# A two-block network on one core: attention of the second block regrouped by head pair, and its PSUM banks dealt out anew

## The chip, the cores and the metric

The kernel runs on one core of one Trainium2 chip. Its time is the device time of one execution in microseconds (us), and of several executions the median is taken. [...] VectorE (DVE) and ScalarE (ACT) read PSUM and do all element-wise work, and the queue of SyncE (SP) fetches the weights from memory.

## The reference

A first block (gating, dilated attention, and a mixture of 16,384 one-row experts) is followed by the two layers of the second block. The change touches these two layers alone. One layer is, cut to what matters (256 tokens, width 1024, eight heads of 64 in each half):

```python
def hybrid_layer(x, w_in, w_out, ln_g, ln_b, rel_bias, topk):
    proj = jnp.einsum('bsd,dn->bsn', x, w_in)
    qA, kA, vA, gA, qB, kB, vB, gB, qI, kI, wI = jnp.split(proj, SPLIT_POINTS, axis=-1)
    oA = stick_breaking_attention(heads(qA), heads(kA), heads(vA))
    oB = dsa_sparse_attention(heads(qB), heads(kB), heads(vB), qI, kI, wI, rel_bias, topk)
    mix = jnp.concatenate([oA * jax.nn.silu(gA), oB * jax.nn.silu(gB)], axis=-1)
    y = jnp.einsum('bsm,md->bsd', mix, w_out)
    return layer_norm_2(ALPHA * x + y, ln_g, ln_b)
```

Half A ("stick") weighs a key by the sigmoid of its score times a running product over the keys between. Half B ("selected") keeps for each query the 64 keys with the highest index score and takes a softmax over them with a position bias.

## The kernel before, in words

All weights and activations are split into a high and a low part, and each product is three matrix multiplications (L116 to L118: high by high, high by low, low by high). A weight arrives as a unit of 128x1024 (`raw`). ACT rounds it to its high part `uhi` (L98) and DVE subtracts to get the low part `ulo` (L99). Seven buffer pairs for split units are used in turn, so that splitting can run ahead of PE by up to seven units.

Two forms of projection appear. With `w_stationary` the weights are the stationary operand: one unit gives 24 matrix multiplications of 256 columns into one PSUM tile `pp`, which ACT then copies out; `heads_t` (L776 to L781) does this for the index projections and for the queries and keys of both halves, one unit per head pair, and the same loop at L847 to L851 for the gates. With `x_units` the tokens are stationary: one unit gives 12 matrix multiplications of 512 columns, six for each block of 128 tokens (`tb`). The values (`rows`, L798) and the output projection at the end (L935 to L941) are made in this form.

One layer runs in the program as follows: values of half B; index keys and queries; index scores (L821) and the choice of 64 keys on DVE (L834 to L844); the gates; then queries and keys of half B (L860, L861); half B for four head pairs (L863 to L891); queries, keys and values of half A (L895 to L897); half A for four head pairs (L900 to L932); the output projection; and the layer norm by token block (L942 to L964), which in the first layer also transposes the result for the next one (L960, L163).

Half B, for one head pair: scores (L788); mask, add and row maximum on DVE (L871); four exponentials on ACT (L875); scaling on DVE (L879); six transposes (L886); a copy (L888); the product with the values, `weighted` (L795); and `finish`, which multiplies by the gate on DVE (L856) and splits the result into `mh` and `ml` (L98, L99). Half A, for one head pair: scores and mask (L905 to L910); Abs, Exp and Ln on ACT (L913 to L915); one DVE step (L917); a split into `sh` and `sl`; products with a triangle (L923) and with minus one (L926), added onto the scores in the same PSUM tile; Exp (L929); `weighted` (L795); and `finish`.

PSUM in this part: `banks()` gives a tile `mm` of two banks, of which there are two in turn, for scores and transposes alike. The rest is three single banks `pp` and one bank `po` for the result of `weighted`. The output projection has four accumulators of one bank, for two halves of the columns (`n`) by two token blocks: those of `n` = 0 are the two banks of one `mm` tile, those of `n` = 1 are two `pp` tiles (L935, L936).

```python
            bk = banks()
            acc4 = [[bk[:, tb, :] for tb in range(2)], [ps_b.tile([128, 512], F32, name="pp") for _ in range(2)]]
```

The order of each engine's instructions is fixed when the program is built. A planner walks the instructions in program order with costs of its own and lets a later one pass one that would still wait, so that the order on an engine isn't the program's. [...]

Of the kernel before, what the change touches and what calls it, by code (L numbers as in the profile page):

```python
# [9 lines left out]
F32 = mybir.dt.float32  # L10
# [5 lines left out]
AF = mybir.ActivationFunctionType  # L16
ALU = mybir.AluOpType
AX = mybir.AxisListType
PSUM = bass.MemoryType.PSUM
# [5 lines left out]
KD = 8  # L25
# [13 lines left out]
def kernel(  # L39
# [146 lines left out]
    def w_stationary(ps, xh, xl, src, eng=V):  # L186
        hi, lo = unit(src, eng)
        for k in range(KD):
            s = slice(k * 128, (k + 1) * 128)
            end = mm3(ps, hi[:, s], lo[:, s], xh[:, k, :], xl[:, k, :], k == 0, k == KD - 1)  # L190
        return end
# [540 lines left out]
    with ExitStack() as c4:  # L732
        p2 = c4.enter_context(tc.tile_pool(name="p2", bufs=1))
        w2 = c4.enter_context(tc.tile_pool(name="w2", bufs=2))
        ps_m = c4.enter_context(tc.tile_pool(name="ps_m2", bufs=2, space=PSUM))


        def banks():
            return ps_m.tile([128, 2, 512], F32, name="mm")

        for tb in range(2):
            bk = banks()
            for n in range(2):
# [10 lines left out]
        cv.close()  # L754
        ps_b = c4.enter_context(tc.tile_pool(name="ps_b2", bufs=3, space=PSUM, side="right"))
        cur = x2
# [15 lines left out]
        for layer in range(2):  # L772
            blk = [0]
            qI = p2.tile([128, 4, T], F32, name="qI", tag="q")

            def heads_t(dst, scale=1.0, func=AF.Copy):  # L776
                for j in range(dst.shape[1]):
                    pp = ps_b.tile([128, T], F32, name="pp")
                    w_stationary(pp, xh, xl, w_t[layer, blk[0]])
                    blk[0] += 1  # L780
                    S.activation(out=dst[:, j, :], in_=pp, func=func, scale=scale)  # L781
# [8 lines left out]

            def weighted(po, v, hp, w):
                for sb, t in ((0, slice(0, 256)), (1, slice(128, 256))):
                    for e in range(2):
                        h = 2 * hp + e
                        P.matmul(out=po[64 * e:64 * e + 64, t], lhsT=v[:, sb, h * 64:(h + 1) * 64],  # L795
                                 rhs=w[:, e, 256 * sb:256 + 128 * sb], start=(sb == 0), stop=(sb == 1))

# [11 lines left out]
            with tc.issue_after(x_ready):  # L809
                heads_t(kI[:, None, :])  # L810
            pw = ps_b.tile([128, 512], F32, name="pp")[:, 0:256].rearrange("p (b t) -> p b t", b=2)
# [4 lines left out]
            with tc.issue_after(x_ready):  # L816
                heads_t(qI)


            acc = [w2.tile([128, T], F32, name=f"acc{tb}", bufs=1) for tb in range(2)]  # L820
            for hp in range(4):  # L821
                pss = banks()
                both_heads(pss, qI, hp, lambda s, sl: kI[s, 0:sl])
# [22 lines left out]

            for k in range(KD):  # L847
                pp = ps_b.tile([128, T], F32, name="pp")
                w_stationary(pp, xh, xl, w_t[layer, blk[0]])
                blk[0] += 1  # L850
                S.activation(out=gT[:, k, :], in_=pp, func=AF.Silu)  # L851
            exp_ln_set()

            def finish(k, po):
                mx_ = w2.tile([128, T], F32, name="mix")
                V.tensor_tensor(out=mx_, in0=po, in1=gT[:, k, :], op=ALU.mult)  # L856
                split(mh[:, k, :], ml[:, k, :], mx_)


            heads_t(qB, 0.125)  # L860
            heads_t(kB)  # L861

            for hp in range(4):  # L863
                pss = banks()
                both_heads(pss, qB, hp, lambda s, sl: kB[s, hp, 0:sl])
# [12 lines left out]
                for e, tb, n in each:  # L878
                    V.tensor_scalar(out=sm[:, e, COL[tb]], in0=sm[:, e, COL[tb]], scalar1=ls[:, n:n + 1],  # L879
                                    scalar2=None, op0=ALU.mult)  # L880
                pt = banks()
                for e in range(2):
# [5 lines left out]
                V.tensor_copy(out=pT, in_=pt[:, :, 0:384])  # L888
                po = ps_b.tile([128, T], F32, name="po", bufs=1)
                weighted(po, vB, hp, pT)  # L890
                finish(4 + hp, po)  # L891


            qA = p2.tile([128, 4, T], F32, name="qA", tag="q")
            heads_t(qA, 0.125)  # L895
            heads_t(kA)
            rows(vA, 0)  # L897


            for hp in range(4):  # L900
                z = banks()
                zz = z[:, :, 0:384]
# [22 lines left out]
                for e in range(2):  # L925
# [3 lines left out]
                S.activation(out=aw, in_=zz, func=AF.Exp)  # L929
                po = ps_b.tile([128, T], F32, name="po", bufs=1)  # L930
                weighted(po, vA, hp, aw)
                finish(hp, po)  # L932


            bk = banks()  # L935
            acc4 = [[bk[:, tb, :] for tb in range(2)], [ps_b.tile([128, 512], F32, name="pp") for _ in range(2)]]  # L936
            parts = [(acc4[n] + [4, 2], w_out_2[layer, n * 4 + i], 2 * i)
                     for i, n in ((2, 1), (3, 1), (2, 0), (3, 0), (0, 0), (1, 0), (0, 1), (1, 1))]
            for j in range(4):
                x_units(parts[j:j + 1], mh, ml)  # L940
            x_units(parts[4:], mh, ml)  # L941
            for tb in range(2):  # L942
                bk = banks() if layer == 0 else None
                st = small.tile([128, 2, 6], F32, name="st2")
# [106 lines left out]
```

## Time and profile before

| | |
|---|---|
| median of three runs | 1301.3 us (1301.26 to 1305.01) |
| the profiled execution | 1302.54 us, of which its span 1300.4 us |
| PE busy in the span | 1256.5 us (97%) |
| DVE, ACT busy | 974.0 us (75%), 641.4 us (49%) |
| the second block | from about 953 us to the end |

A busy share is an average over very different stages. The rows below come from the views of the stages that the change touches: stretches in which all of PE's work is projections, stretches in which attention is mixed in, the step from the first to the second layer, and the end. In the timeline a row gives start and length, engine, line, operation, and output and inputs; in square brackets stands how long the engine sat idle before it, and on whom it waited. Rows of PE overlap, since matrix multiplications are pipelined: what one costs is the distance to the next start. A group's row gives count, busy time, mean length of one in ns, and the idle time before them with its releaser.

### The profile page before, as it was taken

The numbers are of one execution on the slowest core, as the hardware profiler recorded it, in microseconds if no ns is written. First come the engines' busy times: TensorE is split into PE (matmuls) and PEld (weight loads), VectorE is DVE, ScalarE is ACT, GpSimd is POOL, SyncE is SP. The second block draws the span as 40 slices with busy tenths as digits, with TensorE's granted clock in tenths as the row PEclk, the third lists the DMA queues.
The fourth block names the chain that finished last, engine by engine and source line by source line (L and its number), as shares of the span: only waits on it lengthen the run. The fifth ranks groups of instructions, "written<-read, shape, count | busy, mean of one in ns | idle before, by whom it ended". The sixth has DMA issues, their size and how long they took to land. (4 is left out here: it accounts for less than half of the span.)

```text
span 1300.4 us, 22723 instructions
## 1 busy us (share of the span) xinstructions
PE 1256.5 (97%) x8888; PEld 1111.3 (85%) x8888; DVE 974.0 (75%) x1907; ACT 641.4 (49%) x1031; POOL 14.8 (1%) x27
## 2 busy tenths in 40 slices
PE   7999999999999999999999999999999999899995
PEld 5777998999999999998888887888879986699874
DVE  6977999944557999989999987655569665667744
ACT  7555554444544444444444446445455546355561
POOL 0001000000000000000000000000000000000000
PEclk9999999999999999999999999999999999899998
DMA  7824454565564545555555558755654532346310
GB/s 254 263 90 133 149 172 165 180 196 187 172 200 164 164 163 163 164 176 169 177 176 177 178 178 285 245 191 184 192 185 148 181 128 91 130 164 196 122 56 32
DMA packets 61818, 219.08 MB, mean 168 GB/s; under 512 B 7064, under 2 KB 8496, under 8 KB 61584
## 3 DMA queue, kind: packets, MB, share of 16 engines
q1 hardware_dynamic: 60272, 213.03, 49.3%
q0 software_dynamic: 1440, 4.62, 1.2%
q8 instruction: 69, 1.13, 0.3%
q14 instruction: 37, 0.30, 0.1%
HBM read 214.33 MB, written 3.16 MB: 167 GB/s over the span
## 5 line engine op out<-in xcount | busy, mean ns | idle before, releaser
L99 DVE TENSOR_TENSOR ulo<-raw,uhi 128x1024 fp32r<-128x1024 f32 x390 | 474.6, 1220 | 180.8 <-ACT uhi L98 180.2
L98 ACT ACTIVATE uhi<-raw 128x1024 fp32r<-128x1024 f32 x390 | 411.3, 1056 | 360.6 <-PE pu L117 205.3
L116 PE MATMUL pu<-xh,uhi 128*128 128x256 f32 x1024 | 293.5, 287 | 2.3 <-ACT ga L462 2.3
L118 PE MATMUL pu<-xh,ulo 128*128 128x256 f32 x1024 | 292.1, 285 | 1.6 <-DVE ulo L99 1.5
L117 PE MATMUL pu<-xl,uhi 128*128 128x256 f32 x1024 | 290.3, 284 | 0.0
L116 PE MATMUL pv<-uhi,wh 128*128 128x512 f32 x512 | 203.6, 398 | 0.0
L118 PE MATMUL pv<-uhi,wl 128*128 128x512 f32 x512 | 200.8, 392 | 0.5 <-DVE wl L99 0.4
L116 PEld LDWEIGHTS pu<-xh,uhi 128*128 128x128 f32 x1024 | 197.0, 192 | 3.9 <-ACT ga L462 3.1
L117 PE MATMUL pv<-ulo,wh 128*128 128x512 f32 x512 | 200.3, 391 | 0.0
L118 PEld LDWEIGHTS pu<-xh,ulo 128*128 128x128 f32 x1024 | 197.1, 192 | 3.3 <-DVE ulo L99 2.6
L117 PEld LDWEIGHTS pu<-xl,uhi 128*128 128x128 f32 x1024 | 197.2, 193 | 0.0
L116 PE MATMUL pp<-xh,uhi 128*128 128x256 f32 x496 | 141.1, 284 | 0.0
L117 PE MATMUL pp<-xl,uhi 128*128 128x256 f32 x496 | 140.5, 283 | 0.0
L118 PE MATMUL pp<-xh,ulo 128*128 128x256 f32 x496 | 140.1, 282 | 0.0
L98 ACT ACTIVATE wh<-ga 128x256 fp32r<-128x256 f32 x128 | 53.0, 417 | 174.5 <-PE pv L117 172.5
L118 PEld LDWEIGHTS pv<-uhi,wl 128*128 128x128 f32 x512 | 96.1, 188 | 23.5 <-DVE wl L99 1.8
L117 PEld LDWEIGHTS pv<-ulo,wh 128*128 128x128 f32 x512 | 96.2, 188 | 20.2
L116 PEld LDWEIGHTS pv<-uhi,wh 128*128 128x128 f32 x512 | 96.1, 188 | 19.8
L116 PEld LDWEIGHTS pp<-xh,uhi 128*128 128x128 f32 x496 | 94.0, 189 | 3.1 <-issue 3.0
L117 PEld LDWEIGHTS pp<-xl,uhi 128*128 128x128 f32 x496 | 93.9, 189 | 1.5 <-issue 1.4
L118 PEld LDWEIGHTS pp<-xh,ulo 128*128 128x128 f32 x496 | 94.0, 190 | 0.7 <-issue 0.7
L659 DVE SCALAR_TENSOR_TENSOR ga<-pg,ga 128x288 f32<-128x288 f32 (+1 forms) x96 | 87.1, 937 | 7.3 <-PE pg L657 7.3
(278 smaller groups left out, 1653.2 us busy)
## 6 DMA issues: line engine op xcount, KB each, us to landing
raw<-in_expert_u_dram SPq DMA_DIRECT2D x128, 512.0 KB, 3.4
raw<-in_expert_v_dram SPq DMA_DIRECT2D x128, 512.0 KB, 3.3
raw<-in_w_t_dram SPq DMA_DIRECT2D x58, 512.0 KB, 3.9
raw<-in_w_out_dram SPq DMA_DIRECT2D x24, 512.0 KB, 3.3
raw<-in_w_in_n_dram SPq DMA_DIRECT2D x16, 512.0 KB, 5.1
raw<-in_w_n_dram SPq DMA_DIRECT2D x16, 512.0 KB, 3.4
raw<-in_w_query_dram SPq DMA_DIRECT2D x12, 512.0 KB, 3.6
raw<-in_w_in_t_dram SPq DMA_DIRECT2D x4, 512.0 KB, 4.5
```

What stands on the lines that cost most here:

```text
L98: S.activation(out=hi, in_=src, func=AF.Copy)
L99: eng.tensor_tensor(out=lo, in0=src, in1=hi.bitcast(F32), op=ALU.subtract)
L116: P.matmul(out=ps, lhsT=lh, rhs=rh, start=start, stop=False)
L117: P.matmul(out=ps, lhsT=lh, rhs=rl, start=False, stop=False)
L118: return P.matmul(out=ps, lhsT=ll, rhs=rh, start=False, stop=stop).ins
L659: V.scalar_tensor_tensor(out=gv, in0=pg, scalar=1.0 / 32768.0, in1=gv, op0=ALU.mult, op1=ALU.mult)
```

## The change

Both halves are taken head pair by head pair in one loop, each behind its own query and key projection: values of A; then for each pair queries and keys of A, `stick`, queries and keys of B, `selected`. `heads_t` takes the place of its units as an argument, so that they can be read out of order.

PSUM is dealt out otherwise. Half A has one two-bank tile for itself (`mm0`) and half B one (`mm1`), each single-buffered. `po` is gone: `weighted` writes its result into the last 128 columns of the two banks that the pair is using, in three pieces of 128 columns for each head instead of one of 256 and one of 128. The bank so freed is a fourth `pp`. All four accumulators of the output projection are now `pp` tiles of their own. Its units come in another order.

```diff
-        ps_m = c4.enter_context(tc.tile_pool(name="ps_m2", bufs=2, space=PSUM))
-        def banks():
-            return ps_m.tile([128, 2, 512], F32, name="mm")
+        ps_m = c4.enter_context(tc.tile_pool(name="ps_m2", bufs=1, space=PSUM))
+        def banks(n):
+            return ps_m.tile([128, 2, 512], F32, name="mm", tag=f"mm{n % 2}")
...
-        ps_b = c4.enter_context(tc.tile_pool(name="ps_b2", bufs=3, space=PSUM, side="right"))
+        ps_b = c4.enter_context(tc.tile_pool(name="ps_b2", bufs=4, space=PSUM, side="right"))
...
-            def heads_t(dst, scale=1.0, func=AF.Copy):
-                for j in range(dst.shape[1]):
+            def heads_t(dst, base, scale=1.0, func=AF.Copy, js=None):
+                for j in (range(dst.shape[1]) if js is None else js):
                     pp = ps_b.tile([128, T], F32, name="pp")
-                    w_stationary(pp, xh, xl, w_t[layer, blk[0]])
-                    blk[0] += 1
+                    w_stationary(pp, xh, xl, w_t[layer, base + j])
                     S.activation(out=dst[:, j, :], in_=pp, func=func, scale=scale)
...
-            def weighted(po, v, hp, w):
-                for sb, t in ((0, slice(0, 256)), (1, slice(128, 256))):
+            def weighted(bk, v, hp, w):
+                po = bk[:, :, 384:512]
+                for n, (tb, sb) in enumerate(((0, 0), (1, 0), (1, 1))):
                     for e in range(2):
                         h = 2 * hp + e
-                        P.matmul(out=po[64 * e:64 * e + 64, t], lhsT=v[:, sb, h * 64:(h + 1) * 64],
-                                 rhs=w[:, e, 256 * sb:256 + 128 * sb], start=(sb == 0), stop=(sb == 1))
+                        P.matmul(out=po[64 * e:64 * e + 64, tb, :], lhsT=v[:, sb, h * 64:(h + 1) * 64],
+                                 rhs=w[:, e, n * 128:(n + 1) * 128], start=(sb == 0), stop=(sb == tb))
+                return po
...
-            heads_t(qB, 0.125)
-            heads_t(kB)
-            for hp in range(4):
-                pss = banks()
+            def selected(hp):
+                pss = banks(1)
...
-                pt = banks()
+                pt = banks(1)
...
-                po = ps_b.tile([128, T], F32, name="po", bufs=1)
-                weighted(po, vB, hp, pT)
-                finish(4 + hp, po)
-            qA = p2.tile([128, 4, T], F32, name="qA", tag="q")
-            heads_t(qA, 0.125)
-            heads_t(kA)
-            rows(vA, 0)
-            for hp in range(4):
-                z = banks()
+                finish(4 + hp, weighted(pt, vB, hp, pT))
+            def stick(hp):
+                z = banks(0)
...
-                po = ps_b.tile([128, T], F32, name="po", bufs=1)
-                weighted(po, vA, hp, aw)
-                finish(hp, po)
-            bk = banks()
-            acc4 = [[bk[:, tb, :] for tb in range(2)], [ps_b.tile([128, 512], F32, name="pp") for _ in range(2)]]
-            parts = [(acc4[n] + [4, 2], w_out_2[layer, n * 4 + i], 2 * i)
-                     for i, n in ((2, 1), (3, 1), (2, 0), (3, 0), (0, 0), (1, 0), (0, 1), (1, 1))]
+                finish(hp, weighted(z, vA, hp, aw))
+            qA = p2.tile([128, 4, T], F32, name="qA", tag="q")
+            rows(vA, 0)
+            for hp in range(4):
+                heads_t(qA, 21, 0.125, js=[hp])
+                heads_t(kA, 25, js=[hp])
+                stick(hp)
+                heads_t(qB, 13, 0.125, js=[hp])
+                heads_t(kB, 17, js=[hp])
+                selected(hp)
+            acc4 = [[ps_b.tile([128, 512], F32, name="pp") for _ in range(2)] for n in range(2)]
+            parts = [(acc4[n] + [0, 6], w_out_2[layer, n * 4 + i], 2 * i)
+                     for i, n in ((0, 0), (0, 1), (2, 0), (2, 1), (1, 0), (1, 1), (3, 0), (3, 1))]
             for j in range(4):
                 x_units(parts[j:j + 1], mh, ml)
             x_units(parts[4:], mh, ml)
             for tb in range(2):
-                bk = banks() if layer == 0 else None
+                bk = banks(tb) if layer == 0 else None
```

## Rows read from the trace of the kernel before

**Rows 1.** The page: busy time of the engines, and one group of instructions.
```profile
PE 1256.5 (97%) x8888; PEld 1111.3 (85%) x8888; DVE 974.0 (75%) x1907; ACT 641.4 (49%) x1031; POOL 14.8 (1%) x27
...
L99 DVE TENSOR_TENSOR ulo<-raw,uhi 128x1024 fp32r<-128x1024 f32 x390 | 474.6, 1220 | 180.8 <-ACT uhi L98 180.2
```

**Rows 2.** Busy time by stretch; the first line names the columns.
```profile
core 0: us, PE busy (x) PEld busy (x) DVE busy (x) ACT busy (x) POOL busy (x), PEclk, DMA share, GB/s
...
1003.30:1026.20 22.90, 22.90 (x194) 22.82 (x193) 14.32 (x15) 11.95 (x17) 0.00 (x0) 1.00 0.64 207
1026.20:1073.20 47.00, 46.66 (x330) 39.62 (x328) 29.55 (x80) 24.36 (x58) 0.00 (x0) 1.00 0.40 132
1073.20:1101.60 28.40, 25.15 (x146) 18.20 (x145) 15.53 (x19) 20.94 (x28) 0.00 (x0) 0.94 0.30 99
...
1114.90:1139.60 24.70, 18.40 (x89) 14.86 (x88) 20.12 (x33) 9.81 (x16) 1.08 (x2) 0.86 0.52 170
...
1179.10:1202.00 22.90, 22.90 (x195) 22.82 (x193) 14.34 (x15) 11.96 (x17) 0.00 (x0) 1.00 0.64 207
...
1249.00:1275.30 26.30, 23.34 (x145) 17.14 (x144) 13.36 (x17) 19.04 (x26) 0.00 (x0) 1.00 0.00 1
...
1288.80:1300.40 11.60, 0.00 (x0) 0.00 (x0) 8.47 (x20) 0.99 (x4) 0.00 (x0) 0.68 0.24 90
```

**Rows 3.** Timeline, PE, end of the second layer's output projection.
```profile
1282.81 0.39 PE L118 MATMUL mm<-uhi,ml 128*128 128x512 f32 x1
...
1286.99 0.39 PE L118 MATMUL mm<-uhi,ml 128*128 128x512 f32 x1
...
1288.39 0.39 PE L118 MATMUL pp<-uhi,ml 128*128 128x512 f32 x1
```

**Rows 4.** The same view, PE alone, three pairs of half B.
```profile
1032.40:1055.50 23.10, 23.03 (x178) 1.00 0.31 103
```

**Rows 5.** Timeline, PE, half A in the second layer.
```profile
1248.98 0.70 PE L905 MATMUL mm<-qA,kA 64*128 64x256 f32 x4
...
1250.16 0.70 PE L905 MATMUL mm<-qA,kA 64*128 64x256 f32 x4
...
1257.43 0.52 PE L923 MATMUL mm<-sl,tri_r 128*128 128x384 f32 x2
1257.78 0.61 PE L926 MATMUL mm<-ab,neg 128*128 128x128 f32 x4
1258.14 0.59 PE L923 MATMUL mm<-sh,tri_r 128*128 128x384 f32 x2
...
1259.29 0.87 PE L795 MATMUL po<-ab,vA 128*64 128x256 f32 x8
...
1260.09 0.62 PE L923 MATMUL mm<-sl,tri_r 128*128 128x384 f32 x2
1260.55 0.61 PE L926 MATMUL mm<-ab,neg 128*128 128x128 f32 x4
1261.09 0.70 PE L905 MATMUL mm<-qA,kA 64*128 64x256 f32 x4
```

**Rows 6.** The same products with the values, their 128-column part.
```profile
1259.78 0.39 PE L795 MATMUL po<-ab,vA 128*64 128x128 f32 x4
```

**Rows 7.** Timeline, DVE, layer norm of the second layer.
```profile
1284.64 0.69 DVE L947 SCALAR_TENSOR_TENSOR x<-x,pp 128x512 f32<-128x512 f32 x1 [7.92 <-PE pp L118]
...
1287.42 1.29 DVE L947 SCALAR_TENSOR_TENSOR x<-x,mm 128x512 f32<-128x512 f32 x2 [1.36 <-PE mm L118]
...
1295.93 1.42 DVE L957 SCALAR_TENSOR_TENSOR x<-x,rs_z,b_l 128x512 f32<-128x512 f32 x2
```

**Rows 8.** Timeline, PE, step from the first layer to the second.
```profile
1120.50 0.88 PE L163 MATMUL mm<-id_t,x 128*128 128x128 f32 x3 [5.59 <-DVE x L957]
1122.28 0.79 PE L116 MATMUL pp<-uhi,xh 128*128 128x512 f32 x1 [0.69 <-ACT xh L166]
```

**Rows 9.** Timeline, DVE, `finish` of a pair of half A, second layer.
```profile
1260.21 0.42 DVE L856 TENSOR_TENSOR mix<-po,gT 128x256 f32<-128x256 f32 x1 [1.09 <-PE po L795]
```

More of the change, by code (lines that the diff above doesn't have):

```diff
@@ L734 @@
         w2 = c4.enter_context(tc.tile_pool(name="w2", bufs=2))
-        ps_m = c4.enter_context(tc.tile_pool(name="ps_m2", bufs=2, space=PSUM))
-        def banks():
-            return ps_m.tile([128, 2, 512], F32, name="mm")
+        ps_m = c4.enter_context(tc.tile_pool(name="ps_m2", bufs=1, space=PSUM))
+        def banks(n):
+            return ps_m.tile([128, 2, 512], F32, name="mm", tag=f"mm{n % 2}")
         for tb in range(2):
-            bk = banks()
+            bk = banks(tb)
             for n in range(2):
@@ L772 @@
         for layer in range(2):
-            blk = [0]
             qI = p2.tile([128, 4, T], F32, name="qI", tag="q")
-            def heads_t(dst, scale=1.0, func=AF.Copy):
-                for j in range(dst.shape[1]):
+            def heads_t(dst, base, scale=1.0, func=AF.Copy, js=None):
+                for j in (range(dst.shape[1]) if js is None else js):
                     pp = ps_b.tile([128, T], F32, name="pp")
-                    w_stationary(pp, xh, xl, w_t[layer, blk[0]])
-                    blk[0] += 1
+                    w_stationary(pp, xh, xl, w_t[layer, base + j])
                     S.activation(out=dst[:, j, :], in_=pp, func=func, scale=scale)
@@ L809 @@
             with tc.issue_after(x_ready):
-                heads_t(kI[:, None, :])
+                heads_t(kI[:, None, :], 0)
             pw = ps_b.tile([128, 512], F32, name="pp")[:, 0:256].rearrange("p (b t) -> p b t", b=2)
@@ L816 @@
             with tc.issue_after(x_ready):
-                heads_t(qI)
+                heads_t(qI, 1)
             acc = [w2.tile([128, T], F32, name=f"acc{tb}", bufs=1) for tb in range(2)]
             for hp in range(4):
-                pss = banks()
+                pss = banks(hp)
                 both_heads(pss, qI, hp, lambda s, sl: kI[s, 0:sl])
@@ L844 @@
                 bsel.append(bs)
[L847 to L851, printed above, removed]
+            heads_t(gT, 5, func=AF.Silu)
             exp_ln_set()
@@ L855, in finish @@
                 mx_ = w2.tile([128, T], F32, name="mix")
-                V.tensor_tensor(out=mx_, in0=po, in1=gT[:, k, :], op=ALU.mult)
+                V.tensor_tensor(out=mx_.rearrange("p (b t) -> p b t", b=2), in0=po,
+                                in1=gT[:, k, :].rearrange("p (b t) -> p b t", b=2), op=ALU.mult)
                 split(mh[:, k, :], ml[:, k, :], mx_)
-            heads_t(qB, 0.125)
-            heads_t(kB)
-            for hp in range(4):
-                pss = banks()
+            def selected(hp):
+                pss = banks(1)
                 both_heads(pss, qB, hp, lambda s, sl: kB[s, hp, 0:sl])
@@ L929 @@
                 S.activation(out=aw, in_=zz, func=AF.Exp)
-                po = ps_b.tile([128, T], F32, name="po", bufs=1)
-                weighted(po, vA, hp, aw)
-                finish(hp, po)
-            bk = banks()
-            acc4 = [[bk[:, tb, :] for tb in range(2)], [ps_b.tile([128, 512], F32, name="pp") for _ in range(2)]]
-            parts = [(acc4[n] + [4, 2], w_out_2[layer, n * 4 + i], 2 * i)
-                     for i, n in ((2, 1), (3, 1), (2, 0), (3, 0), (0, 0), (1, 0), (0, 1), (1, 1))]
+                finish(hp, weighted(z, vA, hp, aw))
[11 more added lines that the diff above has]
+                     for i, n in ((0, 0), (0, 1), (2, 0), (2, 1), (1, 0), (1, 1), (3, 0), (3, 1))]
             for j in range(4):
```

## The prediction

> **What bounds the kernel now.** I read the page first, then busy time by stretch for the second block, then the timelines of PE and DVE where PE is not full. PE is busy 97% of the span [rows 1], so a gain can only come from the places in which PE stands still or is slowed, and the change touches the second block alone. The table by stretch shows where they are [rows 2]. During pure projections (1003.3 to 1026.2) PE is never idle. Under half B (1026.2 to 1073.2) it misses 0.34 us, since the queries, keys and values of half A are projected meanwhile. Under half A (1073.2 to 1101.6, and 1249.0 to 1275.3 in the second layer) it misses 3.25 and 2.96 us: little is left to fill with but the part of the output projection that needs half B alone, and in the first layer the granted clock falls to 0.94 there. At the step between the layers (1114.9 to 1139.6) PE misses 6.3 us, at a clock of 0.86. At the end there are 11.6 us in which PE does nothing.
>
> The last two are read in the layer norm [rows 7, 3]. DVE takes block 0's sum for `n` = 1, a `pp` tile, at 1284.64, right behind its last product. Block 0's sum for `n` = 0 was finished by PE with the product that starts at 1282.81, yet DVE takes it only at 1287.42, after 1.36 us of idling on PE: the moment at which the product started at 1286.99 ends (0.39 us), and that is block 1's. Both blocks' sums for `n` = 0 lie in one `mm` tile, and the read waits for the last write to the tile. So block 0's layer norm, which could run under block 1's products, waits for nearly all of them. In the first layer PE then idles 5.59 us until DVE has block 0 normalised [rows 8].
>
> **The change part by part.** Terms are sums over a layer, from the end of the gates to the last product of the output projection: now 1003.3 to 1114.9, 111.6 us, and 1179.1 to 1288.8, 109.7 us [rows 2].
>
> *Projections.* Same count. A 256-column product costs 22.9/194 = 0.118 us [rows 2], 16 units of 24 make 45.3 us. A 512-column one costs (1288.39 - 1282.81)/24 = 0.2325 us [rows 3], 12 units of 12 make 33.5 us.
>
> *Half B* among projections: 23.1 us hold three pairs, 66 records of attention out of 178 (8 for the scores, 6 transposes, 8 in `weighted` each), so 112 projections, 13.2 us; 9.9/3 = 3.3 us a pair, four make 13.2 us [rows 4]. It stays among projections.
>
> *Half A* now lies among projections too, which the trace doesn't show. Back to back a pair costs 1.18 us for scores and mask (1248.98 to 1250.16), 0.35 for each of the two triangle products, 0.36 for minus one and 0.80 for `weighted`, 3.05 in all [rows 5]. Below, interleaving adds nothing. For the other end, the same minus-one products cost 0.54 where another shape follows (1260.55 to 1261.09), 0.18 more [rows 5]; four groups a pair, 0.7 us. I take 3.75, because the groups will stand alone; four make 15.0 us.
>
> *`weighted` in three pieces.* Now four records of 256 columns and four of 128 take 0.49 and 0.31 us (1259.29, 1259.78, 1260.09) [rows 5, 6]; then twelve of 128. The columns are as many, so the lower end is no cost. At 0.31/4 = 0.078 each they take 0.94, 0.14 more; at the 256-column price of 0.122 they would take 1.47, 0.67 more, 10.7 us over 16 calls. I take the row of the same shape: 1.1 us a layer.
>
> The sum is 45.3 + 33.5 + 13.2 + 15.0 + 1.1 = 108.1 us, a gain of 3.5 in the first layer and 1.6 in the second. What may stand still in between: at least nothing, at most what half A loses today, about 3 us a layer [rows 2]. I take 0.7, twice the 0.34 us of half B, now that two halves run so. **The stage gains 3.7 us.** All of half A's stall goes, but its interleaving and the smaller pieces take back most of it.
>
> What hides the moved work: a pair's four units and both halves give PE 11.3 + 3.3 + 3.75 + 0.14 = 18.5 us. A half's chain, from scores to `finish`, takes 11.2 us for A (1248.98 to 1260.21, with two pairs in flight) [rows 5, 9]. For B no single row has it; pairs follow each other every 7.7 us in two tiles [rows 4], so it is at most 15.4. From 1003.3 to 1101.6 DVE is busy 59.4 of 98.3 us and ACT 57.3 [rows 2], so about 60%, and this work now has the 74 us of the loop and 11 us of values, some 70%: neither becomes the bound. Single banks cost nothing as long as a chain fits into 18.5 us. After the last keys, PE has the output units of pairs 0 and 1 of both halves (four units, 11.2 us), block 0's share of two more (2.8 us), and half B's own 3.3 us, a part of half A's included some 18 us, against a chain of 15.4 at most. So I expect no hole ahead of the last units, and block 0's products to end 24 steps, 5.6 us, before block 1's. SP's fetches keep their count, and in the pure stretch they run at 207 GB/s with PE full [rows 2], so reordering them costs nothing.
>
> *Accumulators in four tiles.* Block 0's sums can now be read as each ends, 7.0 and 5.6 us before PE's end E. DVE's work in the last layer norm is 1.4 us (two steps of 0.69) and then 1287.42 to 1297.35, 11.3 us, 5.65 a block [rows 7]. Block 0 is then done near E - 1.3 and block 1 by E + 4.3; I add 1.0 for the waits on ACT's root, which the two blocks' steps now hide for each other: E + 5.3. Now DVE ends 8.6 us after E (1288.8 to 1297.35). **The end gains 3.3 us**, and the 3.05 us of the last store stay. Between the layers PE can transpose block 0 before E, and starts about 0.5 us after it, where it now idles 5.59 + 0.69 us [rows 8]; after 5.6 us of products for block 0 it then waits some 2.4 us for block 1. That is ready near E + 8.5: to the 5.3 come block 0's two low parts (0.69 each, as steps of that size), a unit's (1.22 [rows 1]), and 0.6 for transposes and copy (estimates). 6.3 - 2.9 = 3.4 us, and about 1.7 for the lower clock (0.86 over 24.7 us, half of it in the hole itself) [rows 2]. **The step gains 5.1 us.** Bounds of the two together: nothing, if DVE's order keeps them late, and 13 us, if all of the idling of [rows 8] and half of DVE's end go.
>
> The rows show a read that waits for a write to another bank [rows 7, 3]. [...]
>
> **Sum.** 3.7 + 3.3 + 5.1 = 12.1 us. The profiled execution took 1302.5 us, the median of the runs is 1.2 lower. 1302.5 - 12.1 - 1.2 = 1289.2 us.
>
> **Rivals.** *(a) Slower: the single banks.* A pair's scores now wait until `finish` has read the last pair's result out of the same banks, where `po` had one for itself and scores had two tiles. For it: ACT and DVE take split units in between, in fixed order, 1.22 us each on DVE [rows 1]; one ahead of each of eight steps would make the 11.2 us some 21. Against it: half B's chains run among projections with 0.34 us lost [rows 2]. Beyond 18.5 us each further us costs 4 pairs x 2 layers = 8, so that the gain of 12.1 is gone at 20.0 us; at 21 the time is 1289.2 + 20 = 1309. In the row that has such holes today, half A of the first layer, the clock is 0.94 over 28.4 us, in the second layer it is 1.00 with as much idling [rows 2]. [...]
>
> *(b) The layer norm keeps its place.* If the planner puts block 1's ready units ahead of block 0's last ones, the sums of block 0 end 2.8 us before E instead of 5.6. Then half of 8.4 is left, 1293.4. For it: now too the order at the end differs from the program's (a `pp` row is last, and `mm` of block 1 just before it) [rows 3].
>
> *(c) The wait isn't the shared tile's.* Then only the stage gains: 1297.6. Against it stands the coincidence of 1286.99 + 0.39 with 1287.42 [rows 3, 7].
>
> *(d) Interleaving is free and nothing stands still:* half A at 3.05, no 0.7, no cost of `weighted`: 5.6 + 1.4 + 2.2 = 9.2 us more, 1280.
>
> **Chances and range.** The forecast, 1285 to 1293: 0.55. (b) 0.19, (c) 0.09, (a) 0.09, (d) 0.08. The range takes in (b), (c) and the near half of (d): 1282 to 1298. It leaves out (a) and the far half of (d), 0.13. Faster by over 0.3% (3.9 us, about what a measurement here can tell from no change) are the forecast, (b), (d) and a part of (c): 0.85. (c)'s rest and weak forms of (a) give 0.07 for within 0.3%, (a) gives 0.08 for slower.
>
> **What would show it.** Stage: gates' end to E some 108 us in both layers, half A without idle PE above 0.5 us, and clock 1.00 throughout. Tiles: DVE's first L947 (new lines differ) about 7 us before E, and its idle no longer ends on the other block's product. Step: PE idle under 3 us in place of 6.3. End: 8.4 us from E to the end of the span. The prediction is wrong if PE waits on `mix` of the pair before (a), if block 0's sums end late (b), or if `weighted` costs over 1.2 us a call.

## The result, and the profile after

The changed kernel takes 1280.6 us (median of 4 runs, 1279.7 to 1281.4) against 1302.1 us before (4 runs, 1301.3 to 1305.0): a ratio of 0.983, 95% interval 0.981 to 0.985. The direction was forecast, the size was not: the time lies 1.4 us below the range and 8.6 us below the forecast. Where the 21 us come from is read from the stretches of the second block. The first line of page and the table by stretch after (PE, TensorE, makes the matrix products):

```profile
PE 1247.1 (97%) x8952; PEld 1108.9 (87%) x8952; DVE 975.2 (76%) x1907; ACT 641.4 (50%) x1031; POOL 14.8 (1%) x27
```

```profile
core 0: us, PE busy (x) PEld busy (x) DVE busy (x) ACT busy (x) POOL busy (x), PEclk, DMA share, GB/s
1004.60:1022.90 18.30, 18.30 (x109) 16.04 (x108) 12.12 (x14) 10.61 (x13) 0.00 (x0) 1.00 0.64 207
...
1040.25:1057.80 17.55, 17.39 (x156) 16.02 (x154) 11.62 (x26) 11.82 (x23) 0.00 (x0) 1.00 0.36 118
...
1093.05:1108.70 15.65, 15.64 (x68) 12.33 (x66) 10.26 (x18) 6.04 (x8) 0.00 (x0) 1.00 0.34 117
1108.70:1128.60 19.90, 16.93 (x89) 13.38 (x89) 16.97 (x25) 10.20 (x15) 1.09 (x2) 1.00 0.63 223
1166.80:1185.20 18.40, 18.40 (x110) 16.08 (x108) 12.14 (x14) 10.62 (x13) 0.00 (x0) 1.00 0.64 213
1185.20:1255.30 70.10, 69.66 (x580) 62.26 (x579) 45.27 (x98) 44.99 (x88) 0.00 (x0) 1.00 0.29 95
1255.30:1270.90 15.60, 15.59 (x68) 12.33 (x66) 7.56 (x16) 0.92 (x3) 0.00 (x0) 1.00 0.04 13
1270.90:1279.30 8.40, 0.00 (x0) 0.00 (x0) 5.19 (x11) 0.50 (x2) 0.00 (x0) 0.66 0.28 103
```

The stage from the gates' end to the last product E of the output projection runs from 1004.6 to 1108.7 and from 1166.8 to 1270.9, 104.1 us in each layer, where it was 111.6 and 109.7 [rows 2]: a gain of 7.5 and 5.6. PE is full in it. In the four pairs of the second layer it misses 0.44 us of 70.1 where half A alone missed 2.96 us, and the granted clock is 1.00 throughout, also where it was 0.94. The step from E to the index scores of the second layer falls from 37.7 to 31.65 us, and the end from 11.6 to 8.4 us. Gains 13.1, 6.1 and 3.2, in all 22.4; the first block ended 1.3 us later in this execution, so that the span is 21.1 us shorter. Of the stages' 13.1 us, 6.0 are idle time of PE that is gone (3.6 and 3.3 us before, 0.45 in each layer after), 1.7 the clock of layer 1 (3.4 us at a granted 0.50 before, from 1095.1 to 1098.5, half of them counted), and the other 5.4 are PE's work itself grown shorter, 2.7 us a layer.

One pair's period, PE's timeline (scores of half B, half A's products with the values, then half B's six transposes among projections):

```profile
1048.52 0.93 PE L786 MATMUL mm<-kB,qB 64*128 64x128 f32 x8
1049.49 0.88 PE L795 MATMUL mm<-ab,vA 128*64 128x128 f32 x12
1050.30 0.39 PE L118 MATMUL pp<-xh,ulo 128*128 128x256 f32 x1
...
1054.09 0.27 PE L881 MATMUL mm<-id_t,sm 128*128 128x128 f32 x1
1054.12 0.37 PE L116 MATMUL pp<-xh,uhi 128*128 128x256 f32 x1
1054.32 0.49 PE L881 MATMUL mm<-id_t,sm 128*128 128x128 f32 x3
1054.57 0.37 PE L117 MATMUL pp<-xl,uhi 128*128 128x256 f32 x1
1054.78 0.38 PE L881 MATMUL mm<-id_t,sm 128*128 128x128 f32 x2
1054.91 0.36 PE L118 MATMUL pp<-xh,ulo 128*128 128x256 f32 x1
1055.12 0.28 PE L116 MATMUL pp<-xh,uhi 128*128 128x256 f32 x1
```

A period of 17.55 us holds 96 projections at 0.118, so 6.2 us are left for both halves; the forecast had 3.3 + 3.75 + 0.14 = 7.2. From start to start, half B's scores take 0.97 us, `weighted` in three pieces 0.81, and the transposes 1.03 less three projections, 0.68. That is 2.45 us for half B in place of 3.3, and leaves 3.75 for half A, the forecast's figure, but with PE's idle time of 0.16 us a period in it. (The counts are of records: a product of scores or of `weighted` leaves two, a transpose one.)

DVE's layer norm at the end, and PE's step between the layers:

```profile
1263.98 0.69 DVE L943 SCALAR_TENSOR_TENSOR x<-x,pp 128x512 f32<-128x512 f32 x1 [7.22 <-PE pp L118]
...
1265.37 0.69 DVE L943 SCALAR_TENSOR_TENSOR x<-x,pp 128x512 f32<-128x512 f32 x1
...
1271.43 0.67 DVE L943 SCALAR_TENSOR_TENSOR x<-x,pp 128x512 f32<-128x512 f32 x1
...
1274.81 1.41 DVE L953 SCALAR_TENSOR_TENSOR x<-x,rs_z,b_l 128x512 f32<-128x512 f32 x2
```

```profile
1108.29 0.40 PE L118 MATMUL pp<-uhi,ml 128*128 128x512 f32 x1
1109.03 0.63 PE L163 MATMUL mm<-id_t,x 128*128 128x128 f32 x4 [0.34 <-DVE x L953]
1110.35 0.50 PE L116 MATMUL pp<-uhi,xh 128*128 128x512 f32 x1 [0.69 <-ACT xh L166]
...
1111.40 0.66 PE L163 MATMUL mm<-id_t,x 128*128 128x128 f32 x4 [0.32 <-DVE xl L167]
```

Block 0's sums are read 6.9 and 5.5 us before E (1270.9), where the second had waited for block 1's product [rows 7], and DVE ends at 1276.2, E + 5.3. Between the layers PE waits 0.34 us for block 0 where it waited 5.59 [rows 8], and 0.22 us before block 1's first product (1117.83), where the forecast had 2.4.

### The profile page after: what moved, and what is told of

It is laid out like the page before. It is cut to its first block, busy times and chain, and to the rows that moved or that the text cites. A ratio compares the mean times of both kernels' runs of the same rounds, so it can differ in the third digit from the quotient of the medians.

```text
span 1279.3 us, 22833 instructions
## 1 busy us (share of the span) xinstructions
PE 1247.1 (97%) x8952; PEld 1108.9 (87%) x8952; DVE 975.2 (76%) x1907; ACT 641.4 (50%) x1031; POOL 14.8 (1%) x27
## 4 chain that ended last, share of the span: by engine, by line
PE 85%; DVE 8%; ACT 4%; DMA 2%; issue 1%; SPq 0%; DVEq 0%; ACTq 0%
PE pu L116 9%; PE pv L116 9%; PE pu L118 9%; PE pu L117 9%; PE pv L118 9%; PE pv L117 9%; PE pp L118 7%; PE pp L117 7%; PE pp L116 7%; DVE ulo L99 3%; PE pg L656 1%; PE pg L657 1%; ACT uhi L98 1%; PE mm L795 1%; PE rt_ps L116 1%
```

## The experiments

Each was run against the kernel before on the same chip. In the table the stage is taken from the start of ACT's last Silu of each layer, 1.1 us behind the gates' end, to E; the step runs from E to the index scores, the end from E to the end of the span. All are of one profiled execution each; the ratio is that of the times of several.

| | ratio to before (95%) | stage, layer 1 / 2 | step | end |
|---|---|---|---|---|
| before | 1 | 110.5 / 108.5 | 37.7 | 11.6 |
| changed | 0.983 (0.981 to 0.985) | 103.0 / 103.0 | 31.7 | 8.4 |
| accumulators alone | 0.992 (0.990 to 0.994) | 106.3 / 106.2 | 37.2 | 8.8 |
| changed, accumulators shared | 0.990 (0.988 to 0.991) | 103.0 / 103.0 | 37.1 | 11.6 |
| pairs on the old banks | 0.991 (0.989 to 0.992) | 102.9 / 102.9 | 37.1 | 11.6 |
| new banks, old order | 1.009 (1.007 to 1.012) | 117.2 / 117.3 | 36.9 | 11.9 |
| halves apart | 0.992 (0.990 to 0.994) | 107.7 / 106.1 | 35.7 | 9.5 |
| old order of units | 0.982 (0.980 to 0.984) | 103.0 / 103.0 | 31.6 | 8.1 |
| three pieces alone | 1.001 (1.000 to 1.002) | 110.5 / 108.6 | 37.8 | 11.6 |
| six together | 0.984 (0.981 to 0.986) | 103.0 / 102.9 | 31.8 | 8.4 |
| half B on one tile | 0.998 (0.997 to 0.999) | 107.9 / 108.8 | 37.7 | 11.6 |
| products among transposes | 0.987 (0.986 to 0.989) | 106.8 / 106.9 | 35.0 | 8.4 |
| products among scores | 0.991 (0.989 to 0.993) | 107.8 / 107.8 | 33.9 | 8.4 |
| scores side by side | 0.981 (0.980 to 0.983) | 102.6 / 102.7 | 31.7 | 8.4 |

### Which part gives what

*The accumulators alone*, on the kernel before:

```diff
-            bk = banks()
-            acc4 = [[bk[:, tb, :] for tb in range(2)], [ps_b.tile([128, 512], F32, name="pp") for _ in range(2)]]
+            acc4 = [[ps_b.tile([128, 512], F32, name="pp"), ps_b.tile([128, 512], F32, name="po", bufs=1)],
+                    [ps_b.tile([128, 512], F32, name="pp") for _ in range(2)]]
```

> The kernel before with one thing changed: the four accumulators of the output projection lie in four tiles of a bank each (the fourth in the bank of po). My theory, the wait for the shared tile: the step between the layers gains about 6.1 us and the end about 3.2 us as in the changed kernel, so some 9 us less than before, about 1293; DVE takes block 0's first sum 4 to 7 us before the last product, not 1.4. Rival, the wait is not the shared tile's: no change, and the gains at the two ends in the changed kernel come from the new order of the units or of the pairs. Third case: the old order of the units keeps block 0's sums late, a gain of some 4 to 6 us.

*Shared again*, on the changed kernel: the first of those two lines back, with `banks(0)`, and the tiles for the transposes between the layers exchanged (`banks(1 - tb)`), so that block 0's don't need the tile that the accumulators hold.

> The changed kernel with block 0's and block 1's accumulators for n = 0 back in one two-bank tile, all else as changed. If the shared tile is what costs: about 9 us slower than the changed kernel, 1290, and DVE's read of block 0's n = 0 sum waits again for block 1's product. Rival: about the same as the changed kernel, 1281, the gains at the ends come from the order.

*The pairs on the old banks*: the changed loop and order of units, and all of PSUM, where the results of all of PE's products lie here, as before (two rotating `mm`, `po`, three `pp`, shared accumulators, `weighted` in two pieces).

```diff
-        ps_m = c4.enter_context(tc.tile_pool(name="ps_m2", bufs=1, space=PSUM))
+        ps_m = c4.enter_context(tc.tile_pool(name="ps_m2", bufs=2, space=PSUM))
...
-            acc4 = [[ps_b.tile([128, 512], F32, name="pp") for _ in range(2)] for n in range(2)]
+            bk = banks(0)
+            acc4 = [[bk[:, tb, :] for tb in range(2)], [ps_b.tile([128, 512], F32, name="pp") for _ in range(2)]]
```

> The regrouping pair by pair with the new order of the output units, on the old banks: two rotating tiles that both halves share, po in a bank of its own, three pp, the two n = 0 accumulators in one tile, the old two pieces for the weighted values. If the gain of the stage comes from the order of the work: the stage from the gates' end to the last product takes about 104 us in each layer as in the changed kernel, the ends gain nothing, so about 1289. Rival, the banks of each half are needed for it: with the tiles shared, one half's scores wait for the other's chain, the stage takes 108 us or more, 1296 or more.

The second and the third came out as the theories had it. The regrouping alone gives the whole gain of the stage without a bank dealt out anew; putting two accumulators back into one tile costs 0.7% of the time, 5.5 us of the step and 3.2 us of the end. In that run DVE reads block 0's sum for `n` = 0 again only when block 1's products into the same tile are done:

```profile
1268.96 0.69 DVE L944 SCALAR_TENSOR_TENSOR x<-x,pp 128x512 f32<-128x512 f32 x1 [8.13 <-PE pp L118]
...
1273.13 1.29 DVE L944 SCALAR_TENSOR_TENSOR x<-x,mm 128x512 f32<-128x512 f32 x2 [2.75 <-PE mm L118]
```

The first hit its sum, 10 us, but from other places. The end gains 2.8 us, the step 0.5, and the stage, of which nothing was expected, 4.2 and 2.4. By stretch (the stage of each layer, and 20 us behind E):

```profile
1003.80:1110.10 106.30, 105.21 (x713) 89.09 (x712) 65.42 (x122) 61.02 (x109) 0.00 (x0) 1.00 0.42 134
...
1110.10:1130.10 20.00, 15.16 (x61) 11.84 (x61) 15.05 (x26) 6.85 (x13) 1.08 (x2) 0.83 0.46 156
...
1174.90:1281.10 106.20, 105.09 (x713) 89.01 (x711) 63.24 (x123) 55.20 (x104) 0.00 (x0) 1.00 0.30 99
```

PE stands still for 1.1 us of each stage instead of 3.6 and 3.3, and the clock of layer 1 stays at 1.00, which gives the other 1.7 us there. So most of half A's holes before, which the prediction put down to a lack of filling work, came from the accumulators too. The work was there, but its accumulators had no place: in the kernel before, the first product into the `mm` tile of `n` = 0 comes behind the last read of pair 2 of half A, ACT's Exp that ends at 1097.45, and until then only the two `pp` accumulators could be filled:

```profile
1093.76 0.61 PE L923 MATMUL mm<-sh,tri_r 128*128 128x384 f32 x2 [1.79 <-ACT sh L98]
...
1099.59 0.48 PE L116 MATMUL mm<-uhi,mh 128*128 128x512 f32 x1
```

With the accumulators alone, products for `n` = 0 stand in that hole, and the same wait is 0.21 us. In the step PE still waits 3.67 us for block 0 and 1.17 more, and the clock is 0.83 over the 20 us from E on (an estimated 6.8 of them at 0.50, if it has the two values of the trace before, 1.00 and 0.50). Separate tiles help the step only if DVE gets to them in time: here three splits of 1.22 us stand among and just before block 0's steps on DVE, in the changed kernel one.

### What covers the single banks

*New banks, old order*: the changed kernel with the loops taken apart again, and the old order of the units.

```diff
-            for hp in range(4):
-                heads_t(qA, 21, 0.125, js=[hp])
...
+            heads_t(qB, 13, 0.125)
+            heads_t(kB, 17)
+            for hp in range(4):
+                selected(hp)
+            qA = p2.tile([128, 4, T], F32, name="qA", tag="q")
+            heads_t(qA, 21, 0.125)
+            heads_t(kA, 25)
+            rows(vA, 0)
+            for hp in range(4):
+                stick(hp)
```

> The changed kernel's banks (one two-bank tile for each half, four accumulators apart, the weighted values in the half's own banks) with the old sequence: all of half B, then all of half A, the old order of units. If a pair's chain of 11.2 us must be covered by projections, as the prediction says (covered up to 18.5 us), half A here has too little beside it: its four pairs wait for each other, the stage takes 115 us or more, over 1300 in all, slower than with the accumulators alone in four tiles (1292.7). Rival, one tile a half is enough without covering work: about 1292 as with the accumulators alone.

*The halves apart*: `qB`, `kB` and `selected` pair by pair, then `rows(vA, 0)`, then `qA`, `kA` and `stick` pair by pair.

> The changed kernel with half B's four pairs first and half A's after them, each pair still behind its own projections, the halves not interleaved; banks and units as changed. If what counts is that a chain of 11.2 us finds that much other work: half A has 5.7 us of projections, 3.7 of its own and 4.2 of half B's units of the output projection beside each pair, 13.6 in all, so little is lost, stage 103 to 105, 1281 to 1285. Rival, the halves must alternate: half B's pairs have 5.7 + 2.5 beside a chain of about 10 us and half A's wait for each other, 108 or more, 1290 and up (all of one half ahead of the other, with half A's projections first, gave 1316).

The first is rival (a) come true. Half A's pairs follow each other every 11.0 to 11.7 us in the first layer, the length of a chain with its `finish` (11.2 and 0.42), and PE waits for the pair before:

```profile
1095.42 0.70 PE L893 MATMUL mm<-qA,kA 64*128 64x256 f32 x4 [0.60 <-DVE mix L853]
...
1101.95 0.62 PE L911 MATMUL mm<-sh,tri_r 128*128 128x384 f32 x2 [2.50 <-ACT sh L98]
```

Four of 11.6 us are 46.5; the products of the output projection beside them (84 records, 19.5 us) and half A's own (15.0) fill 34.5. The 12.0 that are left are most of what the stage lost against the changed kernel, 14.2 and 14.3: PE stands still for 9.7 and 7.1 us, and the clock reads 0.79 over 15.3 us of the first layer, 0.90 and 0.77 over 34.0 and 14.5 us of the second, by an estimate 6.8 and 13.7 us at 0.50, which cost half of that. So the prediction's condition, a chain within the work beside it, was right, and the loop met it.

With the halves apart the stage lost 4.7 and 3.2, more than the 0 to 2 of the theory and less than the rival's 5. In the first layer two of the us are at the end, where half A's last chain has nothing more beside it:

```profile
1100.30 0.88 PE L795 MATMUL mm<-ab,vA 128*64 128x128 f32 x12 [0.90 <-ACT ab L917]
1102.22 0.50 PE L116 MATMUL pp<-uhi,mh 128*128 128x512 f32 x1 [1.04 <-ACT mh L98]
```

Idle time is 2.7 and 1.2 us of the two stages, against 0.45. The other 2.4 us in each layer are PE at work for longer on the same products; the last run below comes back to them.

*The old order of the units*, in the changed kernel:

```diff
-            parts = [(acc4[n] + [0, 6], w_out_2[layer, n * 4 + i], 2 * i)
-                     for i, n in ((0, 0), (0, 1), (2, 0), (2, 1), (1, 0), (1, 1), (3, 0), (3, 1))]
+            parts = [(acc4[n] + [4, 2], w_out_2[layer, n * 4 + i], 2 * i)
+                     for i, n in ((2, 1), (3, 1), (2, 0), (3, 0), (0, 0), (1, 0), (0, 1), (1, 1))]
```

> The changed kernel with the output projection's units in the old order (both units of pairs 2 and 3 of half B first, half B's other, half A's last). Theory: the stage stays at 104, since the chain of the last pair is covered as well, but DVE gets block 0's sums behind other work, as in the run with the accumulators alone, where the step between the layers gained only 0.5 us: about 5 us of the step are lost, 1286. Rival, the order of the units doesn't matter once the pairs go one by one: 1280.6. If the last pair's chain isn't covered: a hole of some us ahead of the last units in both layers, 1285 to 1295, to be told from the first by the place of the idle time.

The rival holds: once the pairs go one by one, the order of the units makes no difference. So the order of the units by itself doesn't make the step's missing 5.5 us with the accumulators alone. What goes with them in the traces is when DVE takes block 0's second sum: 5.6 us before E in the changed kernel, with the old units and with the scores side by side (PE then waits 0.34 to 0.37 us for block 0), 4.2 us before E with the halves apart (2.96), 3.8 with the accumulators alone (3.67). From that sum DVE needs 5.9 us, and 7.1 and 7.5 in the last two. With the halves apart PE ends that sum 4.2 us before E; with the accumulators alone it ended it 4.9 us before, and a split stood ahead of it on DVE. Half A's pair is the last one in both, but no run isolated why block 0 comes later.

### Why half B became cheaper

*Three pieces alone*, on the kernel before:

```diff
-                for sb, t in ((0, slice(0, 256)), (1, slice(128, 256))):
+                po = po.rearrange("p (b t) -> p b t", b=2)
+                for n, (tb, sb) in enumerate(((0, 0), (1, 0), (1, 1))):
```

> The kernel before with the product of weights and values in three 128-column pieces instead of one of 256 and one of 128 columns, into the same po tile. The prediction's price: 1.1 us a layer, 2.2 us slower; its upper end 10.7 us slower. What the trace of the changed kernel suggests, that the pieces cost by their columns: no difference, within 0.5 us, and a call takes 0.80 us as before.

A call of `weighted` takes 0.81 us (0.80 before, [rows 5]), and the ratio makes the time 1.2 us longer, with an interval of -0.4 to 2.9. The times alone don't exclude the price of 2.2, but the stages are equal to 0.1 us (110.5 and 108.6, the latter 108.5 before).

```profile
1259.98 0.88 PE L796 MATMUL po<-ab,vA 128*64 128x128 f32 x12
1260.79 0.44 PE L924 MATMUL mm<-sl,tri_r 128*128 128x384 f32 x1
```

*Six together*, in the changed kernel, so that no projections lie between the transposes:

```diff
-                for e, tb, n in each:
-                    V.tensor_scalar(out=sm[:, e, COL[tb]], in0=sm[:, e, COL[tb]], scalar1=ls[:, n:n + 1],
-                                    scalar2=None, op0=ALU.mult)
+                V.tensor_tensor(out=s3, in0=s3, in1=lr.rearrange("p e c -> p (e c)")[:, :, None].to_broadcast([128, 6, 128]),
+                                op=ALU.mult)
```

> The changed kernel with half B's six scalings per pair done by one instruction of 128x768, so that the six transposes of a pair become ready together instead of one after the other. Theory, transposes and scores of half B got cheap because projections lie between them: if the six now follow each other back to back, they go up from about 0.07 to 0.14 us each, half B costs some 0.4 us a pair more, about 3 us over the kernel, 1283 to 1284. Rival, they are cheap for another reason (tiles, order of the halves): no change, 1280.6. If the planner still puts projections between them, nothing is told.

The theory falls. Six transposes back to back cost no more than apart: 1054.17 to 1054.95, less one projection (at the cut), 0.66 us.

```profile
1054.17 0.82 PE L884 MATMUL mm<-id_t,sm 128*128 128x128 f32 x6
...
1054.95 0.28 PE L117 MATMUL pp<-xl,uhi 128*128 128x256 f32 x1
```

Then it is what they stood among before. In three of half B's four pairs, the kernel before ran the next pair's scores, 64 rows deep, between this pair's transposes, on PE and in its weight loads:

```profile
1040.26 0.27 PE L886 MATMUL mm<-id_t,sm 128*128 128x128 f32 x1
1040.46 0.48 PE L788 MATMUL mm<-kB,qB 64*128 64x128 f32 x2
1040.88 0.77 PE L886 MATMUL mm<-id_t,sm 128*128 128x128 f32 x5
1041.57 0.92 PE L788 MATMUL mm<-kB,qB 64*128 64x128 f32 x6
...
1042.64 0.28 PE L117 MATMUL pp<-xl,uhi 128*128 128x256 f32 x1
```

```profile
1040.16 0.14 PEld L886 LDWEIGHTS mm<-id_t,sm 128*128 128x128 f32 x1
1040.46 0.29 PEld L788 LDWEIGHTS mm<-kB,qB 64*128 64x128 f32 x2 [0.16 <-issue]
1040.87 0.53 PEld L886 LDWEIGHTS mm<-id_t,sm 128*128 128x128 f32 x5
1041.57 0.52 PEld L788 LDWEIGHTS mm<-kB,qB 64*128 64x128 f32 x6 [0.17 <-issue]
```

1040.26 to 1042.64, less a projection of 0.12, are 2.26 us for the records of six transposes and eight of scores; apart they take 0.66 + 0.97 = 1.63. The loads show where the time goes: between products of one form the load starts some 0.1 us ahead of its product (1040.16 for 1040.26), under the product before, but at each change between 128 and 64 rows the first load starts together with its product. That gives a change a price: mixed, a pair has four changes, the 0.97 of the scores alone holds the one behind them, so that 0.63 us are for three, 0.21 each.

*Half B on one tile*, on the kernel before, so that scores wait until the pair before is done (all other work goes on taking the two tiles in turn):

```diff
-                pss = banks()
+                pss = banks(1)
...
-                pt = banks()
+                pt = banks(1)
```

> The kernel before with half B kept in one two-bank tile and the old order of all work: a pair's scores can't start until the pair before is done, so scores and transposes of two pairs are no longer interleaved, and one, three and two transposes stand apart between projections. Theory as for the run of six together: scores and transposes of half B lose 2 to 3 us in each layer, in all 4 to 6 us faster than before, 1296 to 1298. Rival, the single tile makes pairs wait for each other (7.7 us a pair against a chain of up to 15): slower than before by several us, or no change.

Faster by 2.9 us (interval 1.2 to 4.4), below the 4 to 6 but not slower: scores and transposes take 0.96 and 0.77 us (the latter from 1041.60 to 1042.72, less three projections), 0.53 less than mixed, six times in all. The stages are 2.6 us shorter in layer 1 and 0.2 longer in layer 2, but the 3.4 us at the lower clock lie in layer 1 before and in layer 2 here (0.98), 1.7 us of time; over both layers the stages gain 2.4 us, while PE stands still for 0.6 us more.

*Two products more* (four records), the pair's first scores again, in two places of the changed kernel; they add work whose result nobody reads:

```diff
                         P.transpose(out=pt[:, e, c], in_=sm[:, e, c], identity=id_t)
+                        if e == 0 and n == 0:
+                            for e2 in range(2):
+                                s = slice(64 * e2, 64 * e2 + 64)
+                                P.matmul(out=pt[:, e2, 384:512], lhsT=qB[s, hp, 0:128], rhs=kB[s, hp, 0:128],
+                                         start=True, stop=True)
```

> The changed kernel with two products more for each pair of half B: its first two score products (64 rows deep, 128 columns) once more, into columns that nobody reads, placed behind the first of the pair's six transposes. They add work that the result doesn't use. Theory, that products over 64 rows among transposes make both dearer (in the kernel before, six transposes and eight scores mixed took 2.16 us, apart 1.6): a pair's transposes with the two products in between take some 0.65 us more than the six alone, 8 pairs 5 us, 1286. Rival, mixing costs nothing: only the two products at the price of a score alone, 0.12 each, 0.24 a pair, 1282.5.

> The same two extra products a pair (again work that the result doesn't use), placed behind the pair's own eight scores instead. By both theories 0.24 us a pair, 1.9 us in all, 1282.5; the difference to the run with them among the transposes is the price of mixing, 3 us by the theory, nothing by the rival. Where the order of the kernel puts other products among transposes, a pair shows the higher price.

Among the transposes, and behind the eight scores:

```profile
1072.10 0.27 PE L880 MATMUL mm<-id_t,sm 128*128 128x128 f32 x1
1072.30 0.49 PE L884 MATMUL mm<-kB,qB 64*128 64x128 f32 x4
1072.72 0.77 PE L880 MATMUL mm<-id_t,sm 128*128 128x128 f32 x5
...
1073.44 0.28 PE L116 MATMUL pp<-xh,uhi 128*128 128x256 f32 x1
```

```profile
1049.25 0.93 PE L786 MATMUL mm<-kB,qB 64*128 64x128 f32 x8
1050.01 0.39 PE L863 MATMUL mm<-kB,qB 64*128 64x128 f32 x4
...
1050.55 0.28 PE L116 MATMUL pp<-xh,uhi 128*128 128x256 f32 x1
```

The first takes 1072.10 to 1073.44 less 0.12, 1.22 us, 0.56 more than six transposes alone (forecast 0.65). The second takes 1.18, 0.21 more than eight scores alone. So two changes cost 0.35 us, 0.17 each. As whole runs the two don't make the comparison they were made for. The second is slower, by 4.8 us a stage: two products more moved the planner, which in two of four pairs of a layer now puts half A's scores among half B's transposes. The first lost 3.9 us a stage, 1.0 a pair, since it also parted scores around `weighted` and left half A's triangle 0.6 us more of waiting in a layer. They also lost 3.4 and 2.2 us in the step: PE waits 3.2 and 2.1 us for the copy of the index keys, where the changed kernel waits 1.3, and the clock reads 0.89 over 15.0 us and 0.88 over 13.8 us there, some 3.4 us at 0.50. ACT makes that copy; why it comes later there stays open.

*Scores side by side*, in the changed kernel:

```diff
-                stick(hp)
                 heads_t(qB, 13, 0.125, js=[hp])
                 heads_t(kB, 17, js=[hp])
-                selected(hp)
+                z = scores_a(hp)
+                pss = scores_b(hp)
+                stick(hp, z)
+                selected(hp, pss)
```

> The changed kernel with the scores of half A and half B of a pair issued one behind the other, after the projections of both, so that there is one change to products over 64 rows for each pair instead of two. If each such change costs 0.1 to 0.2 us: 1 to 1.6 us faster than the changed kernel, about 1279. Rival: both halves' chains now start together and the last ones are less covered, a hole ahead of the last units, slower by 1 to 5 us.

The stages are 0.4 and 0.3 us shorter, without a hole at the end; the ratio, 0.981, can't be told from the changed kernel's 0.983. That is less than the 1 to 1.6 us expected, and less still by the price above: a layer has 16 changes of rows in the changed kernel and 8 here, and eight at 0.17 would be 1.4 us. What the rows alone leave out is a third form, products with 64 columns of weights (`weighted`), whose first load starts together with its product too (at 1043.32, in the kernel before). Changes between any two of the three forms are 38 in a stage before, 26 in the changed kernel and 24 here, and PE's time there, without idling and the lower clock, is 105.2, 102.4 and 102.1 us, some 0.2 us a change. The halves apart, whose products stand among projections without the other half's beside them, have 32, but 104.9 us: the price by change is a rough one, and what else counts wasn't isolated.

## Why the prediction was wrong, by its steps

*The stage* failed: 3.7 us were forecast, 13.1 came. By term, a layer: half A was forecast at 15.0, and 4 x 3.75 came, with PE's idling in it. The mis-sized terms are half B, 13.2 against 4 x 2.45 = 9.8; `weighted`'s 1.1 against nothing, its lower end; and the stall of 0.7 against 0.46, which lies in the 3.75. Projections outside the four periods took 34.0 (104.1 less 70.1), 0.5 more than their 33.5. Together 4.7 us a layer, 9.4 in all, more than the whole miss.

The step that failed is "half B among projections ... 3.3 us a pair ... It stays among projections" [rows 4]. The 3.3 had been taken from a stretch where half B stood not among projections only but among its own next pair's scores. The row groups 178 records and hides that; the timeline of the same 23 us shows it. Of the 0.85 us a pair, 0.63 (in three pairs of four) are the mixing of products of 64 and of 128 rows, shown by the two prices side by side, by half B on one tile, and locally by the two products put back. The other 0.2 fits the fewer changes to and from projections, as one half's products now follow the other's; the halves apart, which lack that and lose 2.4 us a layer with PE at work, agree, but no run changed it alone.

*The accumulators* were right in mechanism and near in size: end 3.2 (forecast 3.3, DVE's end at E + 5.3 to the tenth), step 6.1 (forecast 5.1). In the step the term that was off is the wait for block 1, 2.4 us in the forecast and 0.22 measured. Two accumulators shared again gave all of it back. That separate tiles end the wait was the author's estimate, which no row of the kernel before shows; the runs show it: with them DVE reads block 0's second sum 5.5 us before E, and with two sums in one tile again it idles 2.75 us on PE's `mm` and reads 1.4 us before E. What was missed: the shared tile also kept units for `n` = 0 from filling half A's holes, 2.4 to 4.2 us a layer, which the new loop would have regained anyway, since the pairs on the old banks have a stage of 102.9.

*The rivals.* (a) needs its condition, and the loop kept clear of it; in the old order the same banks lose 1%. (b) didn't come: block 0's sums are read 6.9 and 5.5 us before E. (c) is excluded by the shared run. (d), "interleaving is free", gave 1280, the right time from the wrong half, by luck: half A did cost about its 3.75 and not 3.05, and half B had been overpriced. The changed kernel has idle time of 0.14 to 0.16 us in three of the first layer's four pairs and shows a clock of 1.00 in all stretches above with PE at work; the 0.94 that (a) names for a stretch with holes isn't seen there.

## What to carry to other kernels

A price read from a stretch holds for its neighbours too: before it is carried to another order, look at the timeline of that stretch for what stands next to the priced work, above all for PE products of another form (other rows, or other columns of weights): a change between 64 and 128 rows cost 0.17 to 0.21 us here. Regrouping chains into one loop lets single buffers suffice as long as each chain finds its own length of other work, and this balance can be added up in advance: here a chain of 11.2 us in a period of 17.55 us left PE 0.16 us of idling, and in the old order, with pairs 11.0 to 11.7 us apart, PE stood still for 9.7 and 7.1 us a stage. Accumulators that end at different times want tiles of their own, which were worth 5.5 us of the step and 3.2 us of the end here; where they take turns with other work's tiles, they also begin only when that work lets one go, in the kernel before at 1099.59, behind a read that ended at 1097.45.

## What was not expected of the hardware

A change between transposes and products of 64 rows cost 0.17 to 0.21 us on PE, and the trace shows the first load of the new form beginning only with its product, while transposes cost 0.11 us each whether projections lay between them or not. Twelve records of 128 columns with 64 columns of weights took 0.81 us, as much as eight of 256 and 128 columns (0.80). With waits of 3.67 and 1.17 us in it, the step with the accumulators alone has a granted clock of 0.83 over 20 us; with waits of 0.34 and 0.69 us it stayed at 1.00. Half a microsecond at a time, the trace of the kernel before shows 1.00 and 0.50 and otherwise only means of the two; at its step, where PE idled 5.59 us up to 1120.50, the clock reads 0.50 from 1119.0 to 1125.8, so that a part of what this hole cost stood after it.
